# Writing out the engine order of a decoder layer's last up unit and its down projection by hand

## The chip, the cores and the metric

The kernel runs on one core of a Trainium2 chip. The metric is the time of one execution on the device, in microseconds (us); the median of the runs counts, and lower is better. The kernel is built with a scheduler that places instructions on the engines by its own estimate of time, except in stretches that are marked to keep the written order.

## The reference, cut to what matters

One hybrid decoder layer on x of 512 tokens by 2048 columns, float32. A token mixer (gated linear attention beside differential attention) comes first; then the gated feed-forward part, on which the change works:

```
def conv_ffn(h, w_ffn_in, conv_w, conv_b, w_ffn_out):
    up = h @ w_ffn_in                                   # 2048 -> 2 * 5632
    a, b = up[..., :D_FF], up[..., D_FF:]
    a = (conv_w[0] * a_pad[:, 0:S] + conv_w[1] * a_pad[:, 1:S + 1]
         + conv_w[2] * a_pad[:, 2:S + 2] + conv_b)      # causal, over tokens
    return (jax.nn.gelu(a, approximate=True) * b) @ w_ffn_out   # 5632 -> 2048

x = x + rmsnorm(f, ffn_post_norm)
```

## The kernel before

**Split products.** Every float32 matrix product is made from three float32r products: an operand is split into a rounded high half (a copy on ScalarE) and the rest (a subtraction on VectorE), and TensorE multiplies high by high, high by low and low by high into the same PSUM bank. A weight granule is 128 partitions by 1024 elements; `granule` splits it (L135 on ScalarE, L136 on VectorE) into one of three slots of a ring of buffers, or for every fourth granule of the down projection into a spare pair (`xhi`, `xlo`). `split` (L148, L149) does the same for activations.

**Seven products instead of eight.** The up projection's groups 1 to 10 and the down projection are done as two-by-two block products in the manner of Winograd. One `Unit` covers one such product, in seven segments of two granules each: x0, z0, y0, z1, x1, y1, y2. The letter is the PSUM accumulator, and each segment has its own sum of activation blocks (a11, s5, s2, s3, a12, s7, a22) and of weight blocks:

- x0 uses block (0,0), loaded into two `rt` tiles. When a granule of it is split, GpSimd issues a DMA that adds block (0,1) into the same tile (`more`, L873): an accumulating load. z0 uses the result.
- y0 adds block (1,1) (`b22`, two `raw` tiles) to it on VectorE (L889). z1 uses `b22` itself, after whose split another accumulating load adds block (0,1) to it; y1 uses that.
- x1 uses block (1,0) (`b21`, two `raw` tiles). y2 uses the `rt` tiles after VectorE has added `b21` (L907).

There are four `raw` and four `rt` buffers. A granule of an up unit takes 24 matmuls of 256 columns (L924 to L926); one of a down unit takes 12 of 512 columns (L1021 to L1023). The outputs go from PSUM to `acc` and `accp` in SBUF: the first by a copy on ScalarE (L1027), later ones by adding on VectorE (L1029).

**The loops.** The last loop of up units runs over groups 1 to 10 and the two branches; `token_sums` forms the sums of the gated product on VectorE (L992) and stores them and the plain blocks to DRAM (`sd`). Ten down units follow, two (`cb` 0 and 1) for each of the five pairs of groups `c`. `prepare(c, n)` loads a stored sum from DRAM into an `st` tile and splits it into `ah` and `al`, which no longer hold the layer's input by then. After the down units `accp` is combined into `acc`, and `last_group` multiplies the one remaining group 0, adds the squares, scales and writes out.

**What sets the order.** In this part of the kernel before, the calls in the code say what depends on what, and the scheduler decides the order on every engine and on SP's DMA queue. Each engine then takes its instructions strictly in that order; one that waits holds up all behind it. Plain loads go through SP's queue, accumulating loads through GpSimd's. The segment order in the code is y0, z1, x1, y1, the next unit's x0, y2, the next unit's z0.

Of the kernel before, what the change touches and what calls it, by code (L numbers as in the profile page):

```python
# [35 lines left out]
def hybrid_layer(ctx: ExitStack, tc: tile.TileContext, x, attn_pre_norm, w_in, w_alpha_up, b_alpha,  # L36
# [10 lines left out]
    def dma(o, i):  # L47
        return nc.sync.dma_start(out=o, in_=i)
# [111 lines left out]
    def bcast_row(tile_ap, row):  # L160
        dma(tile_ap, row.partition_broadcast(P))
# [763 lines left out]
                mm(o, wh, sl[:, :, kk, :], start=False, stop=False, **NOW)  # L925
                mm(o, wl, sh[:, :, kk, :], start=False, stop=kk == HK - 1, **NOW)  # L926

    held = {}

    def up_unit(gi, br):  # L930
        col0 = DFF * br + 512 * gi
        T = [slice(0, 256), slice(256, 512)]
        st = {}

        def block(i, j, g):
            return w_f3[:, HK * i + 4 * g:HK * i + 4 * g + 4, col0 + 256 * j:col0 + 256 * (j + 1)]

        def chain(c):
            return bank(psa if c == "y" else psm)

        def out(seg, b):
            v = b.rearrange("p (n t) -> p n t", n=2)
            if seg == "x0":
                st["p1"] = fp.tile([P, 2, 256], F32, name="p1", tag="p1", bufs=2)
                act(st["p1"], v, AF.Copy)
            elif seg == "z0":
                st["u1"] = pair_tile()
                tt(st["u1"][:, :, T[1]], v, st["p1"], ALU.subtract)
            elif seg == "y0":
                stt(st["u1"][:, :, T[0]], v, -1.0, st["p1"], ALU.mult, ALU.subtract)  # L950
            elif seg == "z1":
                tt(st["u1"][:, :, T[0]], st["u1"][:, :, T[0]], v, ALU.add)
            elif seg == "x1":
                st["u0"] = pair_tile()
                act(st["u0"][:, :, T[0]], v, AF.Copy)
            elif seg == "y1":
                tt(st["u1"][:, :, T[1]], st["u1"][:, :, T[1]], v, ALU.subtract)
                if br == 0:
                    activate(1)
                else:  # L960
                    product(1)
            elif seg == "y2":
                tt(st["u0"][:, :, T[1]], v, st["p1"], ALU.add)
                if br == 0:
                    activate(0)
                else:
                    product(0)
                    token_sums(gi, st["u0"], st["u1"])

        def activate(j):  # L970
            c = held[gi, j] = pair_tile()
            for n in range(2):
                conv(c[:, n, :], st[f"u{j}"][:, n, :], 4 * gi + 2 * j + n)

        def product(j):
            u = st[f"u{j}"]
            tt(u, u, held.pop((gi, j)), ALU.mult)

        return Unit(4, block, up_prods, chain, out)


    def token_sums(gi, u0, u1):
        c, i = (gi - 1) // 2, (gi - 1) % 2
        T = [slice(0, 256), slice(256, 512)]
        a11, a21, a12, a22 = u0[:, :, T[0]], u0[:, :, T[1]], u1[:, :, T[0]], u1[:, :, T[1]]

        def put(n, src):
            dma(sd[c][n][:, i, :].rearrange("p (n t) -> p n t", n=2), src)

        def add(n, x, y, op):  # L990
            t = fp.tile([P, 2, 256], F32, name=n, tag="sum", bufs=2)
            tt(t, x, y, op)  # L992
            put(n, t)
            return t

        put("a11", a11)
        put("a12", a12)
        put("a22", a22)
        s5 = add("s5", a21, a22, ALU.subtract)
        s2 = add("s2", s5, a11, ALU.subtract)  # L1000
        add("s7", a11, a21, ALU.subtract)
        add("s3", s2, a12, ALU.add)


    place = {"a11": (0, 0), "s5": (1, 0), "s2": (0, 1), "s3": (1, 1), "s7": (2, 0), "a12": (3, 0), "a22": (2, 1)}
# [47 lines left out]
    for i, u in enumerate(ups):  # L1053
        nxt = ups[i + 1] if i + 1 < len(ups) else None
        if i == 0:
            u.x0()
            u.z0()
        u.y0()
        u.z1()
        if i == 0:  # L1060
            for h, r in enumerate(s7raw):
                split(up["s7"][0][:, h], up["s7"][1][:, h], r)
        if nxt is None:
            prepare(0, "a11")
        u.x1()
        if nxt is None:
            prepare(0, "s5")
        u.y1()
        if nxt is not None:
            nxt.x0()  # L1070
            u.y2()
            nxt.z0()
        else:
            downs = [down_unit(c, cb) for c in range(NG // 2) for cb in range(2)]
            downs[0].x0()
            prepare(0, "s2")
            u.y2()
    accps = large_tile("accp")
    accp = [accps[:, :D // 2], accps[:, D // 2:]]
    acc = [large_tile(f"acc{t}") for t in (2, 3, 0, 1)]  # L1080
    acc = acc[2:] + acc[:2]
    ssf = [few.tile([P, 4], F32, name=f"ssf{t}") for t in range(NT)]
    downs[0].z0()
    extra[0] = True
    for i, u in enumerate(downs):
        nxt = downs[i + 1] if i + 1 < len(downs) else None
        nc_ = (i + 1) // 2
        first = i % 2 == 0
        last_cb = i % 2 == 1 and nxt is not None
# [10 lines left out]
        if first:  # L1100
            prepare(i // 2, "s7")
        u.x1()
        if first:
            prepare(i // 2, "a22")
        if last_cb:
            prepare(nc_, "a11")
        u.y1()
        if last_cb:
            prepare(nc_, "s5")
        if nxt is not None:  # L1110
            nxt.x0()
        else:
# [4 lines left out]
        if last_cb:  # L1117
            prepare(nc_, "s2")
        u.y2()
        if nxt is not None:  # L1120
            nxt.z0()

    place_w[0] = 0


    def ffn_out_weights(gi, c):
        return [granule(w_y3[:, 4 * gi + 2 * q:4 * gi + 2 * q + 2, 512 * c:512 * (c + 1)], 2,
                        spare={(3, 1): True, (2, 1): "rt", (3, 0): "rt"}.get((c, q))) for q in range(2)]

    def ffn_out_part(us, gr, t, c):  # L1130
        b = bank()
# [18 lines left out]


    def last_group(gi, us):
        gr = ffn_out_weights(gi, 0)
        for t in range(NT):
            ffn_out_part(us, gr, t, 0)
            square(t, 0)
            scale(t, 0)
        gr = {c: ffn_out_weights(gi, c) for c in (1, 2)}
# [40 lines left out]
                rs[t] = rsqrt_mean(ss, D)  # L1199
            finish(3, 0, 1, 2, 3, last=end)  # L1200

    whole = []
    for q, at in enumerate(((3, 1), (0, 0))):
        raw = small_tile("st")
        dma(raw, ud0[:, 2 * q:2 * q + 2, :].rearrange("p n t -> p (n t)"))
        hi, lo = (piece(v, *at) for v in (ah, al))
        split(hi, lo, raw)
        for n in range(2):
            whole.append((hi[:, S * n:S * (n + 1)], lo[:, S * n:S * (n + 1)]))
    last_group(0, whole)  # L1210


# [28 lines left out]
```

## Time and profile before

| | us |
|---|---|
| median of 3 runs | 2167.92 |
| the three runs | 2167.52, 2167.92, 2173.75 |
| span of the profiled execution | 2150.8 |
| TensorE busy in the span | 2112.4 (98%) |
| VectorE busy | 1414.6 (66%) |
| ScalarE busy | 898.3 (42%) |
| GpSimd busy | 199.2 (9%) |

The span runs from the first to the last instruction of one profiled execution; of that execution no other time is shown. The median of the runs lies 17.1 us above the span: what lies around the instructions. The last up unit ends, and the down projection begins, around 1690 us; its matmuls run until about 2098 us, and the last group and the end of the layer take the rest.

In the rows, PE is TensorE's matmuls, PEld its weight loads, DVE VectorE, ACT ScalarE, POOL GpSimd and SP the queue of plain loads. A row of a timeline gives start, duration, engine, line of the code, operation, what it writes and reads, how many are merged, and in brackets how long the engine had been idle before it and what ended that. A row of waits gives who waited for whom: total time, number of times, longest.

### The profile page before, as it was taken

How to read it: one execution, taken by the hardware profiler on the slowest of the kernel's cores; microseconds unless marked ns; L12 is line 12 of the kernel's file. 1: busy time of each engine (PE TensorE's matmuls, PEld its weight loads, DVE VectorE, ACT ScalarE, POOL GpSimd, SP SyncE). 2: the span in 40 equal slices, each digit the busy share in tenths (PEclk: the TensorE clock that was granted, in tenths of full speed). 3: DMA queues.
4: the chain of work that ended last, by engine and by line, in shares of the span. 5: the costliest groups of instructions: out<-in, count | busy, mean ns of one | idle time of the engine just before them, and what ended most of it. 6: DMA issues, size and time to landing. Idle time of an engine off the chain costs nothing.

```text
span 2150.8 us, 31861 instructions
## 1 busy us (share of the span) xinstructions
PE 2112.4 (98%) x13009; PEld 1875.4 (87%) x13009; DVE 1414.6 (66%) x1725; ACT 898.3 (42%) x1162; POOL 199.2 (9%) x242
## 2 busy tenths in 40 slices
PE   7999999999999999999999999999999899999998
PEld 6878888888888889999999999999999778787786
DVE  5345554443444237688777786777778777888887
ACT  4233332333343224344544553544454554443433
POOL 1000000000000001011111111111110111110100
PEclk9999999999999999999999999999999999999999
DMA  6322222223224335455776757667577777676653
GB/s 214 99 75 79 79 69 79 79 79 88 78 80 169 95 128 186 128 119 136 172 172 149 175 139 189 149 157 191 129 172 177 203 229 182 171 195 170 158 167 145
DMA packets 218471, 303.83 MB, mean 141 GB/s; under 512 B 11776, under 2 KB 155572, under 8 KB 216404
## 3 DMA queue, kind: packets, MB, share of 16 engines
q1 hardware_dynamic: 165204, 238.87, 33.4%
q0 software_dynamic: 53120, 62.92, 19.1%
q8 instruction: 102, 1.67, 0.3%
q14 instruction: 45, 0.37, 0.1%
HBM read 273.97 MB, written 27.79 MB: 140 GB/s over the span
## 4 chain that ended last, share of the span: by engine, by line
PE 46%; issue 45%; POOL 4%; DVE 3%; DMA 2%; ACT 1%; POOLq 0%; SPq 0%; DVEq 0%; ACTq 0%
PE bank L189 7%; PE bank L190 7%; PE bank L191 7%; PE bank L173 5%; PE bank L171 5%; PE bank L172 5%; POOL rt L873 2%; PE bank L926 2%; PE bank L925 2%; PE bank L924 2%; POOL raw L873 2%; PE bank L439 1%; PE bank L507 1%; PE bank L538 1%; DVE ring L136 1%
## 5 line engine op out<-in xcount | busy, mean ns | idle before, releaser
L136 DVE TENSOR_TENSOR ring<-raw,ring 128x1024 fp32r<-128x1024 f32 x305 | 371.6, 1221 | 353.8 <-ACT ring L135 344.1
L135 ACT ACTIVATE ring<-raw 128x1024 fp32r<-128x1024 f32 x305 | 323.1, 1060 | 596.6 <-PE bank L191 157.3
L926 PE MATMUL bank<-ah,ring 128*128 128x256 f32 x1280 | 353.7, 276 | 0.8 <-DVE ring L136 0.8
L924 PE MATMUL bank<-ah,ring 128*128 128x256 f32 x1280 | 353.5, 276 | 0.0
L925 PE MATMUL bank<-al,ring 128*128 128x256 f32 x1280 | 353.4, 276 | 0.0
L136 DVE TENSOR_TENSOR ring<-rt,ring 128x1024 fp32r<-128x1024 f32 x221 | 269.0, 1220 | 89.8 <-ACT ring L135 87.9
L135 ACT ACTIVATE ring<-rt 128x1024 fp32r<-128x1024 f32 x221 | 233.1, 1060 | 223.5 <-PE bank L925 146.1
L926 PEld LDWEIGHTS bank<-ah,ring 128*128 128x128 f32 x1280 | 240.3, 188 | 1.2 <-DVE ring L136 1.2
L925 PEld LDWEIGHTS bank<-al,ring 128*128 128x128 f32 x1280 | 240.4, 188 | 0.1
L924 PEld LDWEIGHTS bank<-ah,ring 128*128 128x128 f32 x1280 | 240.3, 188 | 0.1
L189 PE MATMUL bank<-ring,ah 128*128 128x512 f32 x600 | 236.9, 398 | 0.8 <-ACT ah L148 0.8
L190 PE MATMUL bank<-ring,ah 128*128 128x512 f32 x600 | 235.8, 394 | 0.0
L191 PE MATMUL bank<-ring,al 128*128 128x512 f32 x600 | 235.0, 394 | 0.0
L171 PE MATMUL bank<-ah,ring 128*128 128x512 f32 (+1 forms) x512 | 196.2, 383 | 0.0
L173 PE MATMUL bank<-ah,ring 128*128 128x512 f32 (+1 forms) x512 | 194.7, 380 | 0.0
L172 PE MATMUL bank<-al,ring 128*128 128x512 f32 (+1 forms) x512 | 194.5, 380 | 0.0
L1022 PE MATMUL bank<-ring,ah 128*128 128x512 f32 x424 | 166.7, 393 | 7.3 <-DVE ring L136 7.2
L1023 PE MATMUL bank<-ring,al 128*128 128x512 f32 x424 | 165.8, 391 | 0.0
L1021 PE MATMUL bank<-ring,ah 128*128 128x512 f32 x424 | 158.8, 393 | 3.2 <-ACT ring L135 2.4
L191 PEld LDWEIGHTS bank<-ring,al 128*128 128x128 f32 x600 | 113.2, 189 | 24.3 <-DVE al L149 0.3
L189 PEld LDWEIGHTS bank<-ring,ah 128*128 128x128 f32 x600 | 113.1, 189 | 24.2 <-ACT ah L148 1.2
L190 PEld LDWEIGHTS bank<-ring,ah 128*128 128x128 f32 x600 | 113.3, 189 | 23.7 <-DVE ring L136 0.5
(260 smaller groups left out, 4063.6 us busy)
## 6 DMA issues: line engine op xcount, KB each, us to landing
raw<-in_w_in_dram SPq DMA_DIRECT2D x96, 512.0 KB, 3.7
raw<-in_w_ffn_in_dram SPq DMA_DIRECT2D x96, 512.0 KB, 5.1
raw<-in_w_ffn_out_dram SPq DMA_DIRECT2D x48, 512.0 KB, 7.3
rt<-in_w_ffn_in_dram SPq DMA_DIRECT2D x40, 512.0 KB, 6.6
rt<-in_w_ffn_in_dram POOLq DMA_DIRECT2D x40, 512.0 KB, 6.2
raw<-in_w_ffn_in_dram POOLq DMA_DIRECT2D x40, 512.0 KB, 6.8
raw<-in_w_o_dram SPq DMA_DIRECT2D x32, 512.0 KB, 3.7
rt<-in_w_ffn_out_dram SPq DMA_DIRECT2D x20, 512.0 KB, 8.1
```

The lines of the kernel that those rows point to most:

```text
L135: act(hi, raw, AF.Copy)
L136: tt(lo, raw, hi.bitcast(F32), ALU.subtract)
L171: mm(o, wh, ah[:, t0:t1, kk, :], start=st, stop=False)
L172: mm(o, wh, al[:, t0:t1, kk, :], start=False, stop=False)
L173: mm(o, wl, ah[:, t0:t1, kk, :], start=False, stop=sp)
L189: mm(banks[t], ah[:, t, s, :], w[0][:, k, :], start=st, stop=False)
L190: mm(banks[t], ah[:, t, s, :], w[1][:, k, :], start=False, stop=False)
L191: mm(banks[t], al[:, t, s, :], w[0][:, k, :], start=False, stop=sp)
L924: mm(o, wh, sh[:, :, kk, :], start=start and kk == 0 and n == 0, stop=False, **NOW)
L925: mm(o, wh, sl[:, :, kk, :], start=False, stop=False, **NOW)
L926: mm(o, wl, sh[:, :, kk, :], start=False, stop=kk == HK - 1, **NOW)
L1022: mm(b[j], sh[:, o:o + P], w[1][:, q, :], start=False, stop=False, **NOW)
```

## The change

From the last up unit's x1 through the last down unit's y2 the order on TensorE, ScalarE, VectorE and GpSimd is fixed by hand. `run_in_order` goes through the granules of all segments in a list; it splits two granules ahead of the products at first and three from the tenth on, hangs other work on named granules (`hooks`), and switches the ring's offset from 16 to 0 at one granule (`late`), ahead of which only one is split. The order of segments stays. In addition:

- The loads of a down unit's blocks are issued well ahead: `rt` at the unit before's z0, `b22` at its x1, `b21` at its y1. `b21` of the down units goes through GpSimd's queue (as a plain load) instead of SP's.
- The loads and splits of stored sums are hung on granules that lie some segments ahead of their use; a11 and s5 of the first pair are prepared ahead of the fixed stretch.
- The four sums of the last up group are no longer made at the end of the up projection but one by one behind granules of the first down unit.
- The combination of `accp` into `acc` is cut from six additions of 1024 columns into twelve of 512, spread over the last down unit; group 0's activations and its first two weight granules are prepared inside the fixed stretch.

The diff, cut to its core:

```diff
-    def load(src, a):
+    def load(src, a, by=None):
         raw = wpool.tile([P, GR], F32, name="raw", tag="raw", bufs=4)
-        dma(raw.rearrange("p (a b) -> p a b", a=a), src)
+        (by or nc.sync).dma_start(out=raw.rearrange("p (a b) -> p a b", a=a), in_=src)
         return raw
...
-                    token_sums(gi, st["u0"], st["u1"])
+                    sums = token_sums(gi, st["u0"], st["u1"])
+                    if gi < NG - 1:
+                        for f in sums:
+                            f()
+                    else:
+                        late_sums.extend(sums)
...
-    downs[0].z0()
-    extra[0] = True
-    for i, u in enumerate(downs):
...
-        if first:
-            prepare(i // 2, "s3")
-        if i == 6:
-            g3 = large_tile("g3")
-            bcast_row(g3, ffn_post_norm[0])
-        u.y0()
-        if first:
-            prepare(i // 2, "a12")
-        u.z1()
...
-        u.x1()
...
-        u.y1()
...
-        if nxt is not None:
-            nxt.x0()
-        else:
-            for j in range(2):
-                for half, c, op in ((1, 0, ALU.add), (1, 1, ALU.subtract), (0, 1, ALU.subtract)):
-                    dst = acc[2 * half + j].rearrange("p (b c x) -> p b c x", b=2, c=2)[:, :, c, :]
-                    tt(dst, dst, accp[j].rearrange("p (b x) -> p b x", b=2), op)
...
-        u.y2()
-        if nxt is not None:
-            nxt.z0()
+    SOURCE = {"x0": ("a11", "t"), "z0": ("s5", "t"), "y0": ("s2", "t"), "z1": ("s3", "b22"), "x1": ("a12", "b21"),
+              "y1": ("s7", "b22"), "y2": ("a22", "t")}
...
+    def add_t(u, name, g):
+        tt(u.t[g], u.t[g], getattr(u, name)[g], ALU.add)
...
+    def run_in_order(u, order, ahead, last_weights):
+        gran = [(v, seg, g) for v, seg in order for g in range(2)]
+        ready, nxt = {}, [0]
+        extra, at_slot, late = [], slot[0], None
+        for i in range(len(gran)):
+            extra.append(ahead(i) > 2 and (turn[0] + 1 + i) % 4 == 0)
+            if not extra[i]:
+                at_slot = (at_slot + 1) % 3
+                if late is None and at_slot == 0 and i and extra[i - 1]:
+                    late = i
+
+        def make(i):
+            v, seg, g = gran[i]
+            raw = getattr(v, SOURCE[seg][1])[g]
+            turn[0] += 1
+            place_w[0] = 16 if i < late else 0
+            ready[i] = granule(None, v.a, raw, spare=extra[i])
+            j = {"x0": 1, "z1": 1}.get(seg)
+            if j:
+                nc.gpsimd.dma_start(out=raw.rearrange("p (a b) -> p a b", a=v.a), in_=v.block(0, j, g),
+                                    accum_op=ALU.add)
+
+        for i, (v, seg, g) in enumerate(gran):
+            while nxt[0] < len(gran) and nxt[0] <= i + (1 if nxt[0] == late else ahead(i)):
+                make(nxt[0])
+                nxt[0] += 1
...
+            v.prods(v.banks[seg[0]], op, g, ready.pop(i), seg[1] == "0")
+            if g:
+                v.out(seg, v.banks[seg[0]])
+            for f in hooks.pop((v, seg, g), ()):
+                f()
+
+    def down_phase(u):
+        order = [(u, "x1"), (u, "y1"), (downs[0], "x0"), (u, "y2")]
+        for d, v in enumerate(downs):
+            order += [(v, s) for s in ("z0", "y0", "z1", "x1", "y1")]
+            if d + 1 < len(downs):
+                order.append((downs[d + 1], "x0"))
+            order.append((v, "y2"))
...
+        prepare_at(0, "s2", (u, "x1", 0), (u, "y1", 0))
+        prepare_at(0, "s3", (u, "x1", 1), (d0, "x0", 0))
...
+        for d, v in enumerate(downs):
+            c, cb = d // 2, d % 2
+            before = downs[d - 1] if d else u
+            at(before, "x1", 0, lambda v=v: load_b(v, "b22", 1, 1))
+            at(before, "y1", 1, lambda v=v: load_b(v, "b21", 1, 0, nc.gpsimd))
+            if d + 1 < len(downs):
+                at(v, "z0", 1, lambda w=downs[d + 1]: load_unit(w))
+            for g in range(2):
+                at(before, "y2", g, lambda v=v, g=g: add_t(v, "b22", g))
+            at(v, "z1", 0, lambda v=v: add_t(v, "b21", 0))
+            at(v, "x1", 0, lambda v=v: add_t(v, "b21", 1))
+            if cb and d + 1 < len(downs):
+                w = downs[d + 1]
+                prepare_at(c + 1, "a11", (v, "x0", 0), (v, "z0", 0))
+                prepare_at(c + 1, "s5", (before, "y2", 0), (v, "y0", 0))
...
+        for where in ((d0, "z0", 0), (d0, "y0", 0), (d0, "z1", 0), (d0, "x1", 0)):
+            at(*where, lambda: late_sums.pop(0)())
+        e, f = downs[-2:]
+        at(e, "z1", 1, row_g3)
+        at(f, "x0", 0, combine(0, 0))
...
+    with tc.manual_schedule(engines=IN_ORDER):
+        run_in_order(u, order, lambda i: 2 if i < 10 else 3, last_weights)
...
     def last_group(gi, us):
-        gr = ffn_out_weights(gi, 0)
         for t in range(NT):
-            ffn_out_part(us, gr, t, 0)
+            ffn_out_part(us, gr0, t, 0)
```

More of the change, by code (lines that the diff above doesn't have):

```diff
@@ L1063, in hybrid_layer @@
         if nxt is None:
[L1064 removed]
+            break
         u.x1()
[L1066 to L1067 removed]
         u.y1()
[L1069 to L1079 removed]
@@ new lines, in hybrid_layer, with at @@
+        nxt.x0()
+        u.y2()
+        nxt.z0()
+    accp, acc, g3s = [], [], []
+    ssf = [few.tile([P, 4], F32, name=f"ssf{t}") for t in range(NT)]
+    downs = [down_unit(c, cb) for c in range(NG // 2) for cb in range(2)]
+    SOURCE = {"x0": ("a11", "t"), "z0": ("s5", "t"), "y0": ("s2", "t"), "z1": ("s3", "b22"), "x1": ("a12", "b21"),
+              "y1": ("s7", "b22"), "y2": ("a22", "t")}
+    hooks = {}
+    def at(u, seg, g, *fs):
+        hooks.setdefault((u, seg, g), []).extend(fs)
@@ new lines, in load_unit, with load_b, prepare_parts, first @@
+    def load_unit(u):
+        u.t = [load_t(u.block(0, 0, g), u.a) for g in range(2)]
+        u.b22, u.b21 = [], []
+    def load_b(u, name, i, j, by=None):
+        getattr(u, name).extend(load(u.block(i, j, g), u.a, by) for g in range(2))
+    def add_t(u, name, g):
+        tt(u.t[g], u.t[g], getattr(u, name)[g], ALU.add)
+    def prepare_parts(c, n):
+        got = []
+        def first():
+            got.append(small_tile("st"))
+            dma(got[0], sd[c][n].rearrange("p g x -> p (g x)"))
+        def second():
+            split(piece(ah, *place[n]), piece(al, *place[n]), got[0])
+        return first, second
@@ new lines, in prepare_at, with combine, go, whole_parts @@
+    def prepare_at(c, n, load_at, split_at):
+        f, g = prepare_parts(c, n)
+        at(*load_at, f)
+        at(*split_at, g)
+    def combine(cb, k):
+        half, c, op = ((1, 0, ALU.add), (1, 1, ALU.subtract), (0, 1, ALU.subtract))[k]
+        def go():
+            for j in range(2):
+                dst = acc[2 * half + j][:, 1024 * cb + 512 * c:1024 * cb + 512 * (c + 1)]
+                tt(dst, dst, accp[j][:, 512 * cb:512 * (cb + 1)], op)
+        return go
+    whole = []
+    def whole_parts(q, where):
+        got = []
+        def first():
+            got.append(small_tile("st"))
+            dma(got[0], ud0[:, 2 * q:2 * q + 2, :].rearrange("p n t -> p (n t)"))
+        def second():
+            hi, lo = (piece(v, *where) for v in (ah, al))
+            split(hi, lo, got[0])
+            for n in range(2):
+                whole.append((hi[:, S * n:S * (n + 1)], lo[:, S * n:S * (n + 1)]))
+        return first, second
@@ new lines, in late_tiles, with row_g3 @@
+    def late_tiles():
+        accps = large_tile("accp")
+        accp.extend((accps[:, :D // 2], accps[:, D // 2:]))
+        four = [large_tile(f"acc{t}") for t in (2, 3, 0, 1)]
+        acc.extend(four[2:] + four[:2])
+    def row_g3():
+        g3s.append(large_tile("g3"))
+        bcast_row(g3s[0], ffn_post_norm[0])
+    def run_in_order(u, order, ahead, last_weights):
[22 more added lines that the diff above has]
+                nxt[0] += 1
+            op = SOURCE[seg][0]
+            if g == 0 and seg[1] == "0":
+                v.banks[seg[0]] = v.chain(seg[0])
+            if i + 2 >= len(gran):
+                last_weights(i + 2 - len(gran))
+            v.prods(v.banks[seg[0]], op, g, ready.pop(i), seg[1] == "0")
[3 more added lines that the diff above has]
+                f()
@@ new lines, in hybrid_layer, with last_weights, ffn_out_granule, ffn_out_weights @@
+    order = down_phase(ups[-1])
+    u = ups[-1]
+    u.b21 = [load(u.block(1, 0, g), u.a) for g in range(2)]
+    for n in ("a11", "s5"):
+        prepare(0, n)
+    gr0 = []
+    def last_weights(q):
+        place_w[0] = 0
+        turn[0] += 1
+        gr0.append(ffn_out_granule(0, 0, q, turn[0] % 4 == 0))
+    def ffn_out_granule(gi, c, q, spare=None):
+        return granule(w_y3[:, 4 * gi + 2 * q:4 * gi + 2 * q + 2, 512 * c:512 * (c + 1)], 2, spare=spare)
+    def ffn_out_weights(gi, c):
+        return [ffn_out_granule(gi, c, q, {(3, 1): True, (2, 1): "rt", (3, 0): "rt"}.get((c, q))) for q in range(2)]
```

80 lines of the change are left out of this document (35 added, 45 removed).

## The prediction

> **What bounds the kernel now.** I read the page first: the busy shares, then the chain that ended last.
>
> ```profile
> span 2150.8 us, 31861 instructions
> PE 2112.4 (98%) x13009; PEld 1875.4 (87%) x13009; DVE 1414.6 (66%) x1725; ACT 898.3 (42%) x1162; POOL 199.2 (9%) x242
> PE bank L189 7%; PE bank L190 7%; PE bank L191 7%; PE bank L173 5%; PE bank L171 5%; PE bank L172 5%; POOL rt L873 2%; PE bank L926 2%; PE bank L925 2%; PE bank L924 2%; POOL raw L873 2%; PE bank L439 1%; PE bank L507 1%; PE bank L538 1%; DVE ring L136 1%
> ```
>
> TensorE is busy 98% of the span, so the change can win little. But the chain also runs through L873, the accumulating loads on GpSimd's queue: in the last part something besides TensorE sets the pace. The waits of TensorE from 1684 us on name what it lacks there, the low half of a weight granule (L136):
>
> ```profile
> PE bank L1022 <- DVE ring L136: 7.2, 6, 4.6
> PE bank L1021 <- ACT ring L135: 2.4, 4, 1.0
> PE bank L1022 <- DVE xlo L136: 2.0, 4, 0.8
> ```
>
> The 4.6 is one stall, where the down projection begins. The timeline there:
>
> ```profile
> 1688.05 0.63 PE L1021 MATMUL bank<-ring,ah 128*128 128x512 f32 x2
> 1689.82 1.06 ACT L148 ACTIVATE ah<-st 128x1024 fp32r<-128x1024 f32 x1 [3.35 <-DMA st<-sd0s]
> 1690.91 1.22 DVE L149 TENSOR_TENSOR al<-st,ah 128x1024 fp32r<-128x1024 f32 x1 [3.18 <-ACT ah L148]
> ...
> 1693.33 0.50 PE L1022 MATMUL bank<-ring,ah 128*128 128x512 f32 x1 [4.65 <-DVE ring L136]
> ...
> 1697.54 0.40 PE L1022 MATMUL bank<-ring,ah 128*128 128x512 f32 x1
> ...
> 1900.18 0.39 PE L1021 MATMUL bank<-ring,ah 128*128 128x512 f32 x1
> ...
> 1902.22 0.39 PE L1021 MATMUL bank<-ring,ah 128*128 128x512 f32 x1
> ```
>
> VectorE stood at a split of stored sums (L149) whose load had not landed, and the weight split queued behind it came late. After the gap eleven intervals between matmul starts, from 1693.33 to 1697.54, took 4.21 us. Undisturbed, nine take 2.04 (1900.18 to 1902.22), 0.227 each, so eleven need 2.50. The stall costs 4.65 and another 1.7: 6.3 us.
>
> The floor of a down unit: three matmul lines, each 424 + 136 = 560 times, over ten units: 168 matmuls a unit, 38.1 us.
>
> ```profile
> L1021 PE MATMUL bank<-ring,ah x424: 388/389/632, 1688.0 to 2096.7; 128*128 128x512 f32 x142
> L1021 PE MATMUL bank<-xhi,ah x136: 387/389/503, 1724.2 to 2098.1; 128*128 128x512 f32 x136
> 1868.00:1946.00 78.00, 76.45 (x335) 62.48 (x335) 66.12 (x72) 35.06 (x36) 9.45 (x8) 1.00 0.69 182
> ```
>
> (The last row is a stretch of two units: TensorE 76.45 busy, VectorE 66.12, GpSimd 9.45.) What the units really take is read from GpSimd's second accumulating load of each pair, rt for x0 to z0, raw for z1 to y1, and from the ScalarE split that waited for it:
>
> ```profile
> 1856.43 1.19 POOL L873 DMA_DIRECT2D rt<-in_w_ffn_out_dram  x1 [2.29 <-DVE xlo L136]
> 1934.52 1.19 POOL L873 DMA_DIRECT2D rt<-in_w_ffn_out_dram  x1 [2.29 <-DVE xlo L136]
> 1958.92 1.19 POOL L873 DMA_DIRECT2D raw<-in_w_ffn_out_dram  x1 [2.29 <-DVE xlo L136]
> 1973.03 1.20 POOL L873 DMA_DIRECT2D rt<-in_w_ffn_out_dram  x1 [1.14 <-DVE ring L136]
> 1996.60 1.19 POOL L873 DMA_DIRECT2D raw<-in_w_ffn_out_dram  x1 [2.83 <-DVE ring L136]
> 2013.74 1.19 POOL L873 DMA_DIRECT2D rt<-in_w_ffn_out_dram  x1 [2.29 <-DVE xlo L136]
> ```
> ```profile
> 1944.71 1.06 ACT L135 ACTIVATE xhi<-rt 128x1024 fp32r<-128x1024 f32 x1 [4.69 <-DMA rt<-in_w_ffn_out_dram]
> 1966.95 1.06 ACT L135 ACTIVATE xhi<-raw 128x1024 fp32r<-128x1024 f32 x1 [4.57 <-DMA raw<-in_w_ffn_out_dram]
> 1982.34 2.01 ACT L135 ACTIVATE ring<-rt 128x1024 fp32r<-128x1024 f32 x2 [2.42 <-DMA rt<-in_w_ffn_out_dram]
> 2006.53 1.06 ACT L135 ACTIVATE ring<-raw 128x1024 fp32r<-128x1024 f32 x1 [5.04 <-DMA raw<-in_w_ffn_out_dram]
> ```
>
> Four units from 1856.43 to 2013.74 are 157.3 us, 39.3 each: 1.2 above the floor. They run in a loop: load for z0 (10.2 and 9.3 us from issue to the split that waits), then work on ScalarE and VectorE until the load for y1 is issued (1944.71 to 1958.92 and 1982.34 to 1996.60: 14.2, 14.3), that load (8.0, 9.9), and work until the next x0 load (6.1, 7.2).
>
> **The change, part by part.** Sums are against the profiled span, 2150.8; the median of the runs, 2167.92, lies 17.1 above it, and I add 17.1 back.
>
> *The start.* a11 and s5 of the first sums are now split before the fixed stretch, s2 two granules ahead of x0. The stall at 1688 has no cause left: −6.3. What could be late next is s2's split, which stands between the two weight splits of x0; bounds 0 and −6.3, and I take −6.3, as two weight granules are then ahead. Once, where the ring's offset changes, only one granule is ahead for 2.7 us of matmuls (twelve at 0.227), which holds a split of 1.06 on ScalarE and 1.23 on VectorE (rows below): 0, at most those 2.3. The built program follows the written order on four engines, so that the change does what it says; SP's order is still the scheduler's.
>
> *The loop.* Durations for it, start to start, from VectorE and ScalarE behind the landing at 1944.71:
>
> ```profile
> 1945.80 1.23 DVE L136 TENSOR_TENSOR xlo<-rt,xhi 128x1024 fp32r<-128x1024 f32 x1 [2.20 <-ACT xhi L135]
> 1947.06 1.23 DVE L889 TENSOR_TENSOR rt<-rt,raw 128x1024 f32<-128x1024 f32 x1
> 1948.20 1.22 DVE L136 TENSOR_TENSOR ring<-rt,ring 128x1024 fp32r<-128x1024 f32 x1
> 1949.34 1.28 DVE L1029 TENSOR_TENSOR acc<-acc,bank 128x512 f32<-128x512 f32 x2
> 1950.54 1.22 DVE L907 TENSOR_TENSOR rt<-rt,raw 128x1024 f32<-128x1024 f32 x1
> ...
> 1957.41 1.22 DVE L136 TENSOR_TENSOR xlo<-raw,xhi 128x1024 fp32r<-128x1024 f32 x1
> ```
> ```profile
> 1948.40 1.06 ACT L135 ACTIVATE ring<-rt 128x1024 fp32r<-128x1024 f32 x1 [0.74 <-DVE rt L889]
> ```
>
> ScalarE start to VectorE's low half: 1.09 (1944.71 to 1945.80). One full VectorE operation: 1.14 (1947.06 to 1948.20). A pair of outputs from PSUM: 1.20 (1949.34 to 1950.54). Add to the ScalarE split that needs it: 1.34 (1947.06 to 1948.40). Last low half to load issue: 1.51 (1957.41 to 1958.92).
>
> The built program of the change orders VectorE behind z0's second landing so: low half of z0, add b22 to the first block, its low half for y0, two outputs of y2, add b22 to the second block, its low half, one split of sums, low half of z1's first block, two outputs of z0, low half of z1's second block. Both adds now stand behind the late low half, and each sends ScalarE and VectorE through one round trip; before, the first add was done ahead of the landing. Sum: 1.09 + 1.14 + 1.34 + 1.09 + 1.14 + 1.20 + 1.34 + 1.09 + 1.14 + 1.14 + 1.14 + 1.20 + 1.51 = 15.6, against 14.2. Behind y1's second landing: low half, add b21, low half of x0, two outputs of x1, low half of x0's second block: 1.09 + 1.14 + 1.14 + 1.14 + 1.20 + 1.51 = 7.2, against 6.1 and 7.2.
>
> So a unit takes the larger of 38.1 and 22.8 plus two landings. The four landings above are 10.2, 8.0, 9.3, 9.9, mean 9.4. x1's two loads leave SP's queue and queue behind the x0 loads on GpSimd's, so a little less competes; I take 9.0 (ends 8.0 and 10.2, for those that the trace shows). 22.8 + 18.0 = 40.8, 1.5 over today's 39.3. Eight periods beyond the first: +12.0.
>
> *x1's loads on GpSimd.* Two more issues of 1.19 us a unit, ahead of nothing until z1's loads, six granules on: 9.45 busy in 78 us grows by 4.8. Free while GpSimd has that room.
>
> *The first unit.* Its loads meet the stores of the last sums and the row of gains; a period at 10.2 a landing is 22.8 + 20.4 = 43.2, some 2.4 over the steady one: +2.4, bounds 0 and +5.
>
> *Late sums, the combination, the last group's first weights.* Four half-size adds spread, twelve half-size additions for six full ones (12 at 0.60 against 6 at 1.14: 7.2 and 6.8 us): VectorE has 11.9 us idle in 78 of a stretch, which hides them; without that cover 0.4. The last group's weights are split a little earlier: bounds −1 and +2, taken as 0.
>
> Sum: −6.3 + 12.0 + 2.4 = +8.1. Span 2158.9, time **2176.0**.
>
> **The rivals.** *TensorE paces it (faster).* If two landings stay under 38.1 − 22.8 = 15.3, 7.7 each, no unit waits: eight periods give back 1.2 each, 9.6, and with the start 2150.8 − 6.3 − 9.6 = 2134.9, time 2152. For it: loads now issued far ahead, fewer rivals on SP's queue; against it: the shortest of the four second landings is 8.0.
> The Trainium skill (DMA: Bandwidth & Descriptors, "Queues, rings and completion order") has each DMA engine take turns between the queues that have work. By that rule x1's loads, behind the accumulating ones in one queue, take no turn from them, which is this rival; no run here shows it yet.
>
> *No difference.* Landings at 8.0 to 8.5: 22.8 + 16.5 = 39.3, the units as today. −6.3 + 2.4: time 2164; with 0.3 more a landing, 2169.
>
> *Much slower.* Every landing at 10.2: 43.2 a unit, 3.9 over today, 31 us in eight; −6.3 + 31 + 2.4: 2195. It decides from landings of 9.6 on. For it: rows of 10.2 and 9.9; against it: 8.0 in the same unit.
> The Trainium skill (TensorE: Matmul & The Clock Gate, "Part 1") halves the clock after about 3.4 us idle. By it such units, if they lose their 5.1 in one piece, would each add the 1.7 us seen at 1693; the trace agrees at that one place.
>
> **How the numbers follow.** About 0.3%, 6.5 us, is what a measurement can tell from no change. Forecast (landings 8.7 to 9.6, 2171 to 2186): 0.45, of which 0.05 falls within the 6.5 us. Much slower: 0.12. No difference: 0.20. Faster: 0.23. Faster by over 0.3% is 0.23, within 0.20 + 0.05 = 0.25, slower 0.40 + 0.12 = 0.52. The range 2153 to 2192 leaves out about one in ten on each side; the forecast's own is 2171 to 2186.
>
> **What would show it.** In the profile after: no wait over 1 us of the first down matmuls; from one second rt load to the unit's next, 40 to 41 us; ScalarE idle before z0 and y1 splits until a DMA; TensorE waiting once or twice a unit for VectorE's low half. It is wrong if that period is 38.1 to 38.5 (landings under 7.7), or if the start still holds a stall of 4 us.

## The result and the profile after

| | before | after |
|---|---|---|
| median, first comparison (6 and 6 runs) | 2168.46 | 2178.27 |
| ratio, with its 95% interval | | 1.0040 (1.0021 to 1.0059) |
| repeated (35 and 12 runs) | 2159.1 | 2171.74 |
| ratio, with its 95% interval | | 1.0032 (0.9986 to 1.0077) |

The ratio is formed without runs far above their kernel's quickest, so that it is not the quotient of the medians. The first comparison shows the changed kernel slower, by 0.4%; the interval of the second, at 0.3%, does not exclude that it costs nothing. In the changed kernel the down matmuls are L1026 to L1028, their outputs L1034, the additions of b22 and b21 L1093, the accumulating loads L1167, the plain loads L102 and the last group's matmuls L1267 to L1269. The head of the page after, and its first down matmul:

```profile
span 2170.4 us, 31832 instructions
PE 2133.5 (98%) x13009; PEld 1895.3 (87%) x13009; DVE 1417.7 (65%) x1731; ACT 898.1 (41%) x1162; POOL 214.6 (10%) x262
```
```profile
1707.51 0.40 PE L1026 MATMUL bank<-ring,ah 128*128 128x512 f32 x1
```

This execution took 2172.13 us, so only 1.7 us lie around the span, and in no later run more than 2.2. The kernel before cannot have 17.1 us there: its profiled execution, of span 2150.8, was simply a quicker one than the three runs of its table. The spans differ by 19.6 us, and yet from the first down matmul to the last instruction both traces take the same: 2150.8 − 1688.05 = 462.8 before, 2170.4 − 1707.51 = 462.9 after. All but 0.1 of the 19.6 us lies ahead of that, in the up projection, which the change does not touch but for its last unit. The busy times of the stretch from 1300 to 1500 us, first before, then after, then a second profile of each (columns: stretch, length, then busy time and instructions of PE, PEld, DVE, ACT and POOL, granted clock, DMA share, GB/s):

```profile
1300.00:1500.00 200.00, 199.57 (x1759) 199.18 (x1758) 152.58 (x156) 94.28 (x103) 28.01 (x22) 1.00 0.69 165
```
```profile
1300.00:1500.00 200.00, 200.00 (x1701) 200.00 (x1700) 148.17 (x151) 90.57 (x97) 25.45 (x20) 1.00 0.67 160
```
```profile
1300.00:1500.00 200.00, 200.00 (x1700) 200.00 (x1700) 148.99 (x151) 90.47 (x97) 26.73 (x21) 1.00 0.67 158
```
```profile
1300.00:1500.00 200.00, 199.51 (x1760) 199.31 (x1759) 152.66 (x155) 95.03 (x103) 28.03 (x22) 1.00 0.70 168
```

TensorE is busy all the time at a granted clock of 1.00, and still does 1760 matmuls in 200 us or only 1700. Matmul starts stand 113.3 or 117.8 ns apart (the expectations below say 112.7 and 117.7, from a coarser count). Both kernels have both paces: before 113.3 and then 117.8, after 117.8 and then 113.3. A whole up projection at 117.8 takes 785.9 us instead of 760.0. The times fit that: of all 120 runs of the kernel before, 48 lie between 2140.7 and 2152.9, 72 between 2158.3 and 2176.5, none between. Of its two traced executions one stands in each group (the quicker with 1.7 added to its span); that the pace parts the others too is read from this and from the medians of the groups, 23 us apart.

So like must be compared with like: the first profile before with the second after (113.3), the second before with the first after (117.8 from 1111 us on). The table gives TensorE's lost time from the first down matmul on: the start-to-start intervals of all its matmuls, less 226.7 ns for each (113.3 for the up matmuls among them).

| lost, us | before, 113.3 | after, 113.3 | before, 117.8 | after, 117.8 | predicted difference |
|---|---|---|---|---|---|
| first 24 down matmuls | 6.6 | 0.1 | 4.6 | 0.2 | −6.3 |
| next 168 (first unit) | 6.4 | 3.3 | 6.9 | 0.7 | +2.4 |
| eight units more | 7.9 | 20.6 | 1.8 | 17.6 | +12.0 |
| the rest | 2.7 | 7.0 | 2.2 | 5.4 | 0 |
| sum | 23.6 | 31.0 | 15.5 | 23.9 | +8.1 |
| first down matmul to end | 462.8 | 470.0 | 454.7 | 462.9 | |

In these four traces the change costs 7.2 us at the one pace and 8.2 at the other. The equal stretches of the first pair of traces were two differences that cancelled.

### The profile page after: what moved, and what is told of

The parts are those of the page before. It is cut to its first block, busy times and chain, and to the rows that moved or that the text cites. A ratio compares the mean times of both kernels' runs of the same rounds, so it can differ in the third digit from the quotient of the medians.

```text
span 2170.4 us, 31832 instructions
## 1 busy us (share of the span) xinstructions
PE 2133.5 (98%) x13009; PEld 1895.3 (87%) x13009; DVE 1417.7 (65%) x1731; ACT 898.1 (41%) x1162; POOL 214.6 (10%) x262
## 4 chain that ended last, share of the span: by engine, by line
PE 73%; issue 18%; DVE 3%; POOL 2%; DMA 1%; ACT 1%; POOLq 0%; SPq 0%; DVEq 0%; ACTq 0%
PE bank L925 10%; PE bank L926 10%; PE bank L924 10%; PE bank L189 6%; PE bank L190 6%; PE bank L191 6%; PE bank L173 5%; PE bank L171 5%; PE bank L172 5%; PE bank L439 1%; PE bank L507 1%; POOL raw L1167 1%; PE bank L538 1%; DVE ring L136 1%; POOL rt L1167 1%
## 5 line engine op out<-in xcount | busy, mean ns | idle before, releaser
L136 DVE TENSOR_TENSOR ring<-raw,ring 128x1024 fp32r<-128x1024 f32 x305 | 372.4, 1222 | 349.7 <-ACT ring L135 344.6
L926 PE MATMUL bank<-ah,ring 128*128 128x256 f32 x1280 | 358.2, 280 | 0.0
L925 PE MATMUL bank<-al,ring 128*128 128x256 f32 x1280 | 358.2, 280 | 0.0
L924 PE MATMUL bank<-ah,ring 128*128 128x256 f32 x1280 | 358.2, 280 | 0.0
L136 DVE TENSOR_TENSOR ring<-rt,ring 128x1024 fp32r<-128x1024 f32 x221 | 269.9, 1222 | 114.0 <-ACT ring L135 113.9
L1026 PE MATMUL bank<-ring,ah 128*128 128x512 f32 x424 | 166.8, 393 | 6.2 <-DVE acc L1034 5.9
L1028 PE MATMUL bank<-ring,al 128*128 128x512 f32 x424 | 165.3, 390 | 0.0
L190 PEld LDWEIGHTS bank<-ring,ah 128*128 128x128 f32 x600 | 113.1, 189 | 23.6 <-DVE ring L136 0.5
L189 PEld LDWEIGHTS bank<-ring,ah 128*128 128x128 f32 x600 | 113.0, 189 | 23.6 <-ACT ah L148 0.7
```

The source lines that it names most:

```text
L136: tt(lo, raw, hi.bitcast(F32), ALU.subtract)
L189: mm(banks[t], ah[:, t, s, :], w[0][:, k, :], start=st, stop=False)
L190: mm(banks[t], ah[:, t, s, :], w[1][:, k, :], start=False, stop=False)
L924: mm(o, wh, sh[:, :, kk, :], start=start and kk == 0 and n == 0, stop=False, **NOW)
L1026: mm(b[j], sh[:, o:o + P], w[0][:, q, :], start=start and st == 0, stop=False, **NOW)
```

## The experiments

### Both kernels again

No edit. 

> The kernel before, profiled a second time. In the first two profiles the stretch from the first down matmul to the end is the same (462.8 us before, 462.9 after), and the 19.6 us between their spans lie ahead of it: in the up projection the after profile's matmuls start 117.7 ns apart from 1111 us on, the before profile's 112.7 ns. Theory (pace): the up projection has two paces in either kernel, and which one a run gets is not the change's doing: this profile shows stretches of both paces or a span unlike 2150.8, and its changed stretch is again 461 to 465 us. Rival (the change sets the pace): the kernel before keeps 112.7 ns throughout the up projection, span 2149 to 2153.

> The changed kernel, profiled a second time. Pace theory: its changed stretch is again 461 to 465 us, the period of the down units 40.0, and the rest of the span follows from how long the up matmuls stand 117.7 ns apart (4.4% of that time, some 32 us if it is the whole 745 us from 943 on); ratio to the kernel before 1.002 to 1.006. Rival (the changed stretch is slower in most runs and the one profile was lucky): the stretch is 468 us or more, and the up projection at 112.7.

Measured: the kernel before had span 2167.7, 117.8 ns throughout the up projection, and a stretch of 454.7, where 461 to 465 was expected; the changed kernel had span 2157.7, 113.3, and 470.0. Neither expectation held whole, and the changed kernel's second profile has the signs of its rival (468 or more at the quicker pace). That the pace is not the change's doing is shown: each kernel had each. The stretch differed with the pace, by 8.1 us before and 7.1 after, which I had not expected. Why is open. A slower up projection may give the loads of the first stored sums, and VectorE, time to catch up; but the table gives the start only 2.0 of the 8.1, and the eight units 6.1. Nor does the pace alone settle the stretch: 2152.1 to 2154.0 were measured for three runs of the changed kernel, some 5 to 7 us less than for the one traced at 113.3 throughout (2159.4). The waits of TensorE from 1684 us on, in the second profile before and then the second after:

```profile
PE bank L1022 <- DVE ring L136: 4.8, 4, 2.6
PE bank L1021 <- ACT ring L135: 2.5, 4, 1.0
```
```profile
PE bank L1026 <- DVE acc L1034: 7.0, 10, 1.5
PE bank L1027 <- DVE ring L136: 5.7, 9, 1.1
PE bank L1027 <- DVE xlo L136: 3.0, 5, 0.8
PE bank L1267 <- ACT ring L135: 1.5, 1, 1.5
```

Before, one wait of 2.6 at the start is the longest (4.6 in the first profile). After, none exceeds 1.5 (one of 2.3 in the first profile, at the last unit's end), but there are many, for outputs (L1034) and low halves (L136): VectorE is late in every unit.

### The early addition: the loop's price

```diff
-                at(before, "y2", g, lambda v=v, g=g: add_t(v, "b22", g))
+            at(v, "x0", 1, lambda v=v: add_t(v, "b22", 0))
+            at(before, "y2", 1, lambda v=v: add_t(v, "b22", 1))
```

> The changed kernel with one move: the addition of b22 to the first block's half is written one granule earlier, so that on VectorE it stands ahead of the late low half for z0 instead of behind it. Loop theory (a unit takes 22.8 us of work plus two landings of accumulating loads): one addition and one round trip, 1.34 + 1.14 = 2.5, leave the loop, 20.3 + 2 x 8.6 = 37.5, below the 38.1 of the matmuls; from one second rt load to the next 38.1 to 38.6 instead of 40.0, and the stretch from the first down matmul to the end 11 to 15 us shorter than 462.9. Rival (the landings stretch to whatever time is there, or TensorE's waits come from the order of outputs and splits and not from the loop): the period stays at 39.6 to 40.2, the stretch within 3 us of 462.9.

In this kernel the first down unit's z0 uses a sum that already holds b22, so that it computes something else there, with the same operations. First the loop of the changed kernel at 113.3 ns, GpSimd's second load of each pair and then the ScalarE operations behind the landings:

```profile
1812.69 1.19 POOL L1167 DMA_DIRECT2D rt<-in_w_ffn_out_dram  x1 [0.88 <-DVE ring L136]
...
1934.97 1.19 POOL L1167 DMA_DIRECT2D rt<-in_w_ffn_out_dram  x1 [1.16 <-DVE xlo L136]
...
1959.56 1.21 POOL L1167 DMA_DIRECT2D raw<-in_w_ffn_out_dram  x1 [1.12 <-DVE xlo L136]
...
1975.45 1.19 POOL L1167 DMA_DIRECT2D rt<-in_w_ffn_out_dram  x1 [1.16 <-DVE ring L136]
...
2015.90 1.19 POOL L1167 DMA_DIRECT2D rt<-in_w_ffn_out_dram  x1 [1.16 <-DVE xlo L136]
```
```profile
1944.01 1.06 ACT L135 ACTIVATE xhi<-rt 128x1024 fp32r<-128x1024 f32 x1 [4.01 <-DMA rt<-in_w_ffn_out_dram]
1947.58 1.06 ACT L135 ACTIVATE ring<-rt 128x1024 fp32r<-128x1024 f32 x1 [2.51 <-DVE rt L1093]
1952.34 1.06 ACT L135 ACTIVATE ring<-rt 128x1024 fp32r<-128x1024 f32 x1 [3.70 <-DVE rt L1093]
...
1968.24 1.06 ACT L135 ACTIVATE xhi<-raw 128x1024 fp32r<-128x1024 f32 x1 [3.78 <-DMA raw<-in_w_ffn_out_dram]
```

The unit reads off as: landing 1934.97 to 1944.01, 9.04; work 1944.01 to 1959.56, 15.55; landing to 1968.24, 8.68; work to 1975.45, 7.21: 40.5 in all. Five units from 1812.69 to 2015.90 take 40.6 each. In the 15.55 ScalarE waits twice for an addition (L1093): the two round trips. With the early addition:

```profile
1822.90 1.19 POOL L1167 DMA_DIRECT2D rt<-in_w_ffn_out_dram  x1 [0.88 <-DVE ring L136]
...
1958.54 1.21 POOL L1167 DMA_DIRECT2D raw<-in_w_ffn_out_dram  x1 [1.12 <-DVE xlo L136]
...
2012.98 1.19 POOL L1167 DMA_DIRECT2D rt<-in_w_ffn_out_dram  x1 [1.16 <-DVE xlo L136]
```
```profile
1945.43 1.06 ACT L135 ACTIVATE xhi<-rt 128x1024 fp32r<-128x1024 f32 x1 [3.73 <-DMA rt<-in_w_ffn_out_dram]
1946.39 1.05 ACT L135 ACTIVATE ring<-rt 128x1024 fp32r<-128x1024 f32 x1
```

y0's split now starts right behind z0's, and from the landing's split to the next load it is 1945.43 to 1958.54, 13.11: 2.44 less, where 1.34 + 1.14 = 2.48 was worked out. The period is 38.0 (1822.90 to 2012.98, five units), the floor of the matmuls; the stretch 445.4, 17.5 under the changed kernel's 462.9 at about the same pace, more than the 11 to 15 expected. The rival's 39.6 to 40.2 is out: the loop set the pace, and one addition's place in VectorE's order decides whether it does. Median 2147.28, ratio to the kernel before 0.9947 (0.9903 to 0.9992).

### b21 back on SP's queue

```diff
-            at(before, "y1", 1, lambda v=v: load_b(v, "b21", 1, 0, nc.gpsimd))
+            at(before, "y1", 1, lambda v=v: load_b(v, "b21", 1, 0))
```

> The changed kernel with the two loads of b21 back on SP's queue. If x1's loads on GpSimd's queue take no turn from the accumulating loads while on SP's they would: landings of the second accumulating loads go from about 8.7 to 9.2 us and more, the period from 40.0 to 41 or more, the stretch from the first down matmul to the end 466 to 475. If it makes no difference for them which queue carries b21: period 39.8 to 40.3, stretch 461 to 465. If b21 delays GpSimd's own issues: landings shorter, period 39.5 or less.

```profile
1812.37 1.19 POOL L1167 DMA_DIRECT2D rt<-in_w_ffn_out_dram  x1 [1.15 <-DVE ring L136]
...
2015.40 1.19 POOL L1167 DMA_DIRECT2D rt<-in_w_ffn_out_dram  x1 [1.15 <-DVE xlo L136]
```

The period is 40.6, as in the changed kernel at the same pace (113.3). From issue to the waiting split, the second load for z0 took 9.5 on the mean of six units where it took 9.1, that for y1 8.5 of four where it took 8.6 of five. The stretch, 475.9 against 470.0, was longer than the "no difference" case said: 1.1 of it was lost in the first unit, 1.7 in the eight next, 2.9 behind them. Median 2170.64 against 2171.74. So the period and the landings say that the queue that carries b21 hardly touches the loop; the stretch came out at the upper end of the first case, and why is open: one trace of each does not tell it from chance.

### The early addition in all units but the first, and the tail

```diff
-                at(before, "y2", g, lambda v=v, g=g: add_t(v, "b22", g))
+                where = (v, "x0", 1) if d and g == 0 else (before, "y2", g)
+                at(*where, lambda v=v, g=g: add_t(v, "b22", g))
```

> The early addition again, in every unit but the first, which keeps its order as in the changed kernel (there the second granule ahead is made later, and an addition at the earlier place came before the split that reads the old sum). Loop theory: as with the addition moved in all units, the period is 37.8 to 38.4 and the stretch from the first down matmul to the end 444 to 450 us (439 of matmuls without a wait, plus 5 to 11); against the kernel before at the same pace of the up projection 10 to 16 us less: ratio 0.992 to 0.996. Rival (the first unit's order carried the gain): stretch 455 or more.

Measured: stretch 446.0, the eight units behind the first lose 0.8 us in all instead of 17.6 (both with the up projection ending at 117.8), median 2140.98, ratio 0.9929 (0.9879 to 0.9980). As the loop theory has it.

On top of it, the second kernel of this pair:

```diff
-(((3, 1), (f, "z0", 0), (f, "y1", 0)), ((0, 0), (f, "z1", 0), (f, "y2", 0)))
+(((3, 1), (e, "y1", 1), (f, "z0", 0)), ((0, 0), (f, "z0", 1), (f, "z1", 0)))
...
-{(3, 1): True, (2, 1): "rt", (3, 0): "rt"}
+{(1, 1): True, (2, 1): "rt", (3, 0): "rt"}
```

> The early addition, and two moves in the last unit: the two splits of the last group's stored sums are written some four segments earlier, and the last group's second granule of its second column block goes to a spare tile instead of a ring slot that its first block still reads. Theory of the tail (VectorE and the ring's slots hold back the last group: 7.0 us of waits there in the changed kernel, 2.7 before): the last group's waits fall from 4.3 with the early addition alone to 1 to 2.5, the stretch by 2 to 3.5 us. Rival (it is the landing of the last weights): no more than 0.5 us.

TensorE's waits from 2080 us on with the early addition alone, and in this kernel:

```profile
PE bank L1268 <- ACT ring L135: 1.5, 1, 1.5
PE bank L1269 <- DVE xlo L136: 0.8, 1, 0.8
PE bank L1269 <- DVE ring L136: 0.8, 1, 0.8
```
```profile
PE bank L1026 <- DVE acc L1034: 0.9, 1, 0.9
PE bank L1269 <- DVE xlo L136: 0.8, 1, 0.8
PE bank L1268 <- ACT xhi L135: 0.5, 1, 0.5
```

The wait for a ring slot's split is gone. The time lost behind the eight units is 3.1, against 4.8 with the early addition alone and 5.4 in the changed kernel at this pace: a gain of more than the rival's 0.5, less than hoped. The stretch, 446.2, did not fall, as the first unit lost 2.9 where it lost 1.2 in the other. That is not the edit's doing as far as the traces tell: with other offsets of the weights (below) the same kernel's first unit lost 0.8, 3.4, 0.7 and 0.7. Median 2135.28, ratio to the kernel before 0.9909 (0.9860 to 0.9958): the fastest kernel here, below both. Its step over the early addition alone is not shown in the times.

### The pace of the up projection

`place_w`, the offset of the weight ring in the up projection, is 16 elements in both kernels. Four other values, on the last kernel:

```diff
-            place_w[0] = 16 if i < late else 0
+            place_w[0] = 32 if i < late else 0
```

(and the same in the units ahead of the fixed stretch).

> The kernel of the tail experiment with the up projection's weight ring moved by 32 elements instead of 16. Theory of the pace (two matmul paces in the up projection, 112.7 and 117.7 ns, picked by where weights stand against the other operand in SBUF): one pace alone, below 114 or above 117, in the whole up projection, and the spread of the times (some 30 us) falls to under 10. Rival (the pace is drawn at stalls, whatever the place): the same two paces and the same spread.

> The same with an offset of 8 elements. Theory of place: one pace alone, other than with 16 or 32 perhaps. Rival: the same two paces, 112.7 and 117.7 ns, and a spread of some 30 us.

> The kernel of the tail experiment with an offset of 24 elements. Theory of place: one pace, or a pair, that is a property of the offset: near 118 if odd multiples of 8 are alike (8 gave 118.3), near 113 if 16 is the edge. If it holds 113 in every run: times 2129 to 2137 all through, which would be the fastest kernel here. Rival (no rule of place): two paces 112.7 and 117.7 with a spread of 30 us.

> The same with an offset of 48 elements. Theory of place: if what counts is the remainder by 32, 48 is like 16: two paces, 112.7 and 117.7, spread some 30 us, median 2130 to 2150. If larger offsets are slower (32 gave 120): one pace of 118 to 120, times above 2160.

| offset | matmul starts apart, ns | median | all runs |
|---|---|---|---|
| 8 | 118.3 | 2165.02 | 2162.3 to 2166.4 |
| 16 | 113.3 or 117.8 | 2135.28 | 2130.8 to 2161.3 |
| 24 | 118.7 | 2165.36 | 2157.2 to 2169.3 |
| 32 | 120.0 | 2168.58 | 2165.3 to 2177.3 |
| 48 | 117.8 | 2160.31 | 2152.8 to 2164.5 |

The stretch from 1300 to 1500 us with 32:

```profile
1300.00:1500.00 200.00, 200.00 (x1669) 200.00 (x1668) 145.77 (x147) 90.21 (x98) 25.45 (x20) 1.00 0.65 153
```

The pace depends on where the weights stand, as nothing else was changed. 113.3 was seen only at 16: this kernel's own profile there is at 117.8 throughout, those of the other kernels show 113.3. The other offsets have one profile each (8 has three, all at 118.3), but no time there is as low as 113.3 throughout would make it: 26 to 41 us, by the offset, below that of the profiled run (an estimate from the up projections' lengths in the traces). With 48 the pair of paces that I expected did not show, nor times all above 2160. That a smaller spread goes with one pace is plain for 8, less so for 24, 32 and 48 (some 12 us). In the changed kernel's first profile the change of pace can be seen. TensorE's weight loads there:

```profile
1111.05 0.19 PEld L925 LDWEIGHTS bank<-al,ring 128*128 128x128 f32 x1
1111.21 0.19 PEld L926 LDWEIGHTS bank<-ah,ring 128*128 128x128 f32 x1
1111.32 0.19 PEld L924 LDWEIGHTS bank<-ah,ring 128*128 128x128 f32 x1
```

One load starts 0.16 behind the last instead of 0.11, and from there to the end of the up projection, 595 us on, the starts stand 117.8 ns apart. In two other traces the pace changes from 113.3 to 117.8 at a wait, as if waits drew it anew: of some twenty waits of 0.1 to 1.4 us in the up projections traced at 16, three are followed by 117.8 and the others by 113.3. What decides the draw is open.

### The change with the pace held fixed

Both kernels with an offset of 8 (the edit above, 8 for 16).

> The kernel before with the up projection's weight ring moved by 8 elements instead of 16, where the last call's kernel showed one pace (its twelve times within 4.1 us). With the draw of the pace gone, the change alone is left between this kernel and the next. From the traces at 117.7 ns: stretch from the first down matmul to the end 453 to 457 us, times 2170 to 2177, spread under 8.

> The changed kernel with the same offset of 8. Theory: the change costs 7 to 9 us at either pace (stretch 462.9 against 454.7 at 117.7 ns; 470.0 against 462.8 at 112.7): its median 7 to 10 us above that of the kernel before with offset 8, ratio 1.003 to 1.005, stretch 461 to 465. Rival (the change costs nothing and the pace made the difference of the medians): within 3 us of it.

Before: 12 runs from 2172.86 to 2182.62, median 2178.31: above the 2170 to 2177 expected, and spread by 9.8 instead of under 8. After: 9 runs from 2182.15 to 2185.66, median 2183.63. The difference of the means is 5.5 us, ratio 1.0025 (1.0017 to 1.0033, from the spread of the two sets). The change costs time at a fixed pace too, somewhat less than the 7 to 10 expected; "within 3 us" is out. The stretches of the two profiles, 460.9 and 463.5, stand only 2.6 apart, as the kernel before lost 5.1 in the eight units here where it lost 1.8 at 117.8; its stretch, expected at 453 to 457, was missed by 4. The early addition with the tail edits at this offset (the table's first row) stands 13.7 below the kernel before in the mean, but was measured on another chip.

## Why the prediction was right, and where only by luck

*The total.* The span was forecast as 2158.9; at the pace of the profile it was made against, the changed kernel's is 2157.7. The time, 2176.0, lies 2.3 below the first median and 4.3 above the second. Luck has a part in the span too: two terms were wrong, the first unit by −5.5 and the last group by +4.3, and nearly cancel.

*The 17.1 us around the span: wrong.* 1.7 lie there. The rest was the pace: the profile before was at 113.3, and the median of its three runs, at 2167.92, in the upper cluster of the times. Adding the 17.1 back came out right because the change moves both clusters up by about as much. The upper ones have medians of 2169.4 (72 runs before) and 2177.2 (14 runs after), the lower ones of 2146.4 (48 runs) and 2153.7 (4 runs, the one traced at 113.3 among them). In which of them a median of few runs falls is the draw of the pace; one in the lower would have been near 2154, the edge of my range, with the same change.

*The start, −6.3:* right at the pace of that profile (−6.5), −4.4 at the other. Nothing came late in its place, and the switch of the ring's offset, which lies in the first unit, cost no more than the 0.7 lost there in the first profile after.

*The loop, +12.0:* right in its parts. The work behind z0's landing was put at 15.6 and took 15.55, behind y1's 7.2 and 7.2, a landing 9.0 and on the mean 9.1 and 8.6. The period of 40.8 measured 40.6 (40.0 in the first profile after), and eight units cost 12.7 more, or 15.8 at the other pace. There the kernel before loses next to nothing in its loop (1.8): it stands near TensorE's floor, where small shifts of the landings could decide, which is not shown.

*The first unit, +2.4: wrong in sign.* It lost less than before, by 3.1 or 6.2. I had compared it with a steady unit, as though the first unit before cost nothing extra. The rows for it were in the trace before; GpSimd's second rt loads there:

```profile
1693.57 1.19 POOL L873 DMA_DIRECT2D rt<-in_w_ffn_out_dram  x1 [4.35 <-DVE ring L136]
...
1737.41 1.20 POOL L873 DMA_DIRECT2D rt<-in_w_ffn_out_dram  x1 [0.56 <-DVE ring L136]
```

They stand 43.8 apart, 4.5 more than those of a steady unit. In the second profile after, the same two loads stand 42.7 apart (1687.91 and 1730.62): the 43.2 of the prediction was near, and what it was compared with was wrong.

*The last group, 0 (−1 to +2): undersized.* It lost 4.3 more, or 3.2. VectorE's 11.9 us of idle time in two units, which was to hide the additions and splits, is not where they were put. VectorE in the second profile after, of its eighteen rows in a stretch of the last unit's end the first and the last two:

```profile
2080.12 1.22 DVE L136 TENSOR_TENSOR xlo<-raw,xhi 128x1024 fp32r<-128x1024 f32 x1
...
2098.67 2.35 DVE L136 TENSOR_TENSOR ring<-raw,ring 128x1024 fp32r<-128x1024 f32 x2
2100.95 1.27 DVE L1034 TENSOR_TENSOR acc<-acc,bank 128x512 f32<-128x512 f32 x2
```

None has an idle time ahead of it, from 2080.12 to 2102.22, and TensorE waited 1.5 for an output (L1034) in it. A share of idle time over a stretch hid nothing in the place where the work was hung.

*The rivals.* The landings' means, 9.1 and 8.6 (8.85 together), lie inside the forecast's 8.7 to 9.6, above the 8.0 to 8.5 of no difference and below the 10.2 of the much slower case. TensorE pacing the units needed 7.7 or less; none of the means came near, and the loop reached the floor by losing 2.44 of work instead. The rule behind that rival (the Trainium skill, DMA: Bandwidth & Descriptors, "Queues, rings and completion order": each DMA engine takes turns between the queues with work) was put to the test with b21: 0.4 us for one landing of two, none for the other. The direction agrees for one; at 1.3 needed for each, it does not decide here.

*The clock.* The Trainium skill (TensorE: Matmul & The Clock Gate, "Part 1") has the clock halve after about 3.4 us idle. Units did not lose their time in one piece, and paid no such price. The last group paid it. TensorE in the second profile after, and a stretch of it with the granted clock:

```profile
2111.87 0.39 PE L1269 MATMUL bank<-ring,al 128*128 128x512 f32 x1
2113.79 0.50 PE L1267 MATMUL bank<-ring,ah 128*128 128x512 f32 x1 [1.53 <-ACT ring L135]
2115.05 0.80 PE L1268 MATMUL bank<-ring,ah 128*128 128x512 f32 x1 [0.76 <-DVE ring L136]
2115.64 0.63 PE L1269 MATMUL bank<-ring,al 128*128 128x512 f32 x1
2116.07 0.63 PE L1267 MATMUL bank<-ring,ah 128*128 128x512 f32 x1
```
```profile
2114.80:2118.10 3.30, 3.05 (x7) 2.48 (x8) 3.04 (x5) 0.72 (x2) 0.00 (x0) 0.50 0.00 0
```

Two waits, 1.53 and 0.76, with one matmul between, are followed by starts 0.43 apart and a granted clock of 0.50. Here the trace has the half pace after less idle time than that rule names, and not in one piece. The second profile of the kernel before has it behind a single wait of 2.6 (0.50 from 1716.9 to 1720.2), while one of 2.3 in the first profile after (to 2109.74) left the clock at 1.00.

## What to carry to other kernels

Follow the loop, not the share: two loads that can each be issued only when the work on the last is done set a period of work plus landings, and one addition that stands behind a landing rather than ahead of it was worth 2.4 us a unit. When spans and times of one kernel disagree, or repeat in clusters, count the instructions of an untouched stretch in each trace before reading anything from the difference. Idle time that is to hide moved work must lie at the place to which the work is moved.

## What the runs showed of the hardware

The same stream of 128x256 float32r matmuls, each with its own weight load, runs at 113.3, 117.8, 118.3, 118.7 or 120.0 ns a matmul at a granted clock of 1.00, by the offset of the weights in SBUF. At an offset of 16 elements it has two lasting paces, and in one trace it goes from the quicker to the slower at a weight load that is 0.05 us late, and stays there for 595 us. Between the two lie 26 us of 2150 in a whole up projection, three times what the change itself cost.
